# Picking the first pair's rows as rows: stationary slot matrix, one more turn, and row stores from other buffers

## The chip, the cores and the metric

The kernel runs on one core of one Trainium2 chip. The metric is device time in microseconds (us) of one execution; lower is better. Before the change it is 1299.22 us, the median of 3 runs (1299.15 to 1299.3).

The engines go by the profile's names. PE is TensorE (matmuls; its weight loads are listed as PEld), DVE is VectorE, ACT is ScalarE, POOL is GpSimd, SP is SyncE, which here only issues DMAs. ACTq and SPq are the instruction streams of ACT and SP as far as they issue DMAs. A matmul has a stationary operand, which is loaded into the array, and a moving one, which streams through it. PSUM is the memory that PE writes into.

## The reference, cut to what matters

One decoder layer over a sequence of 512 tokens of width 1024, in float32. Four token mixers run on one input projection, their outputs are gated, merged and put through an output projection, and the residual is added. Then comes a mixture of experts: 4 groups of 8 experts; each token goes to 2 experts of one group.

```
x = x + gate1 * (merged @ w_out)                 # end of the mixer half
h = rms_norm(x) * (1 + scale2) + shift2          # input of the experts
group  = argmax(h @ w_router_group)              # 1 of 4
e1, e2 = top 2 of the 8 experts of that group    # with softmax gates
y = sum over e1, e2 of  gate_e * w_down_e(silu(h @ w_gate_e) * (h @ w_up_e))
x = x + gate2 * y
```

Each of the 32 experts has 6 MB of float32 weights, 198 MB in all, and each is read once whatever the routing.

## The kernel before, in words

Tokens are four blocks of 128 (t = 0 to 3), and `xm` holds the residual, 128 tokens by 1024 columns a block. Two stages touch the change.

**The output projection and the router** (L1271 to L1309) go in two halves of two blocks each (half 0: t = 0, 1; half 1: t = 2, 3). A half makes four column blocks of 256 columns (n = 0 to 3). Each has 48 matmul records `mm` in split precision (high and low parts of weights and activations, `wh`, `wl`, made by ACT at L253 and DVE at L254), then DVE multiplies by the gate into one of two buffers `yo` (L1290), adds it to `xm` (L1291; in half 0 POOL does that), and ACT squares the sum for the norm (L1293, `yo` being its scratch output). `logits` (L1256) then turns the block with four transposes `z` (L1260), ACT copies them from PSUM to `xT` (L1263) and PE makes the router's logits `pl`. In half 1 the products of column blocks 2 and 3 use weights kept from half 0; those of 0 and 1 are converted again.

**`route(half)`** (L1141) starts when a half's logits are there. It first writes normalised rows of x to a scratch in DRAM, `xhd`, from which later pairs gather their tokens: ACT scales `xm` into a buffer (L1157) and issues the store (L1158). Block i = 0 goes through `xg[0]` in one 512 KB store; block i = 1 goes through `yo[0]` and `yo[1]` in two stores of 256 KB. Then DVE works out group, experts, ranks and gates in a long chain of small operations. In half 1, when all 512 tokens are known, it ends with the tables of the first expert pair: `tb` and `tg` are matmuls that turn tokens into slots, `toki` holds the token number of each slot, `gx` the gates. From the last logits of half 1 on PE's order is the written one, and in `route(1)` DVE's is too; elsewhere the scheduler sets both.

**`pick`** (L1111) makes the tokens of pair 0 by matmul, straight from `xm`, so that no store and no gather stand before it. The slot matrix `rp` has, for each slot (64 per expert, 128 per pair), the norm factor at its token. A matmul has 128 columns of `xm` as the stationary operand (every fourth of 512) and `rp` as the moving one; the result is already turned (features by slots) in PSUM, `pt0`. It is called for blocks 0 and 1 in `meanwhile()`, a generator that fills PE's waiting spots in `route(1)` together with dummy matmuls `scr`, and for blocks 2 and 3 at the end, between `tb` and `tg`.

**The experts.** 16 pairs of experts follow. `turn_in(p)` transposes the gathered rows `xg[p % 2]` (L1357) for every pair but the first, whose `pt0` is ready, and scales them into `xe` (L1364, L1366). `front(p)` multiplies with the first two weight matrices (`ph`), `Back` with the third (`py`). `fetch(p)` (L1133) is the indirect DMA on POOL that gathers the rows of pair p. The weights come on SP's queue in loads of 1 MB through a ring of 20 buffers; a load waits until PE is done with the tile that its buffer held. DMAs issued from SP and ACT share eight completion semaphores in turn, so that a load can also wait for the DMA that used its semaphore before, row stores included.

Of the kernel before, what the change touches and what calls it, by code (L numbers as in the profile page):

```python
# [9 lines left out]
F32 = mybir.dt.float32  # L10
# [5 lines left out]
AF = mybir.ActivationFunctionType  # L16
# [5 lines left out]
D = 1024  # L22
KD = D // 128
NT = S // 128
# [8 lines left out]
WARM = (1, 0, 0, 2)  # L33
# [4 lines left out]
def trunk(ctx, tc, x, c, ada_w, ada_b, norm1_g, norm2_g, w_in, hgrn_lb, hgrn_norm_g, conv_w, conv_b, conv_ln_g,  # L38
# [3 lines left out]
    V, A, P, T = nc.vector, nc.scalar, nc.gpsimd, nc.tensor  # L42
# [14 lines left out]
    def mm(o, l, r, start, stop):  # L57
        T.matmul(o, l, r, start=start, stop=stop, skip_group_check=True)  # L58
# [12 lines left out]
    def psm(nm="mm"):  # L71
        return ps_mm.tile([128, 512], F32, name=nm, tag="mm")

    def psz(nm="z2"):
        return ps_z.tile([128, 2, 512], F32, name=nm, tag="z2")
# [194 lines left out]
    a = A.activation(wh[:, 4:], raw[:, 4:], AF.Copy)  # L270
# [690 lines left out]
    xm = keep.tile([128, NT, D], F32, name="xm")  # L961
# [44 lines left out]
    nr = nrm.enter_context(tc.tile_pool(name="nr", bufs=1))  # L1006
    yo = [nr.tile([128, 2, 256], F32, name="yo", bufs=2) for _ in range(2)]
# [26 lines left out]
    xg = [kp.tile([128, D], F32, name="xg0")]  # L1034
# [54 lines left out]
    def stream():  # L1089
        for i in range(len(order)):  # L1090
            load_to(i + len(ring))
            yield loaded[i]
# [15 lines left out]
            V.tensor_tensor(oh, iob, bc(idx), op=OP.is_equal)  # L1108
        return mx, idx, oh

    def pick(ts, ds):  # L1111

        for d in ds:
            a, k = divmod(d, 4)
            for t in ts:
                mm(pt0[:, d], xm[:, t, a * 512 + k:(a + 1) * 512:4], rp[t // 2][:, t % 2], t == 0 and k == 0, t == NT - 1)

    def meanwhile():


        scr = psm("scr")
        for n, ds in zip(WARM, ((), range(4), range(4, 8), ())):
            for _ in range(n):
                mm(scr, ident, xm[:, 0, :512], True, True)
            pick((0, 1), ds)
            a = yield
            if a is not None:
                mm(scr[:a.shape[-1], :2], a, ident[:, :2], True, True)
        yield

    def fetch(p):

        P.indirect_dma_start(out=xg[p % 2], out_offset=None, in_=xhd[:, :],  # L1133
                             in_offset=bass.IndirectOffsetOnAxis(ap=toki[:, p:p + 1], axis=0),
                             bounds_check=S - 1, oob_is_err=False)
# [3 lines left out]
    oR, ev, gv, cr, rp, pt0 = [], [], [], [], [], None  # L1139

    def route(half, pl, between=None):  # L1141

        then = between or (lambda a: None)
        ts = slice(2 * half, 2 * half + 2)
# [6 lines left out]
            V.scalar_tensor_tensor(lg[:, i], pl[:, i * 36:(i + 1) * 36], r[:, i:i + 1], crow, op0=OP.mult, op1=OP.add)  # L1151
        for i in range(2):
            t = 2 * half + i
            for cs, xs in ((slice(0, D), xg[0]),) if not i else ((slice(0, 512), yo[0]), (slice(512, D), yo[1])):
                if i:
                    xs = xs.rearrange("p a b -> p (a b)")
                A.activation(xs, xm[:, t, cs], AF.Copy, scale=r[:, i:i + 1])  # L1157
                nc.scalar.dma_start(xhd[t * 128:(t + 1) * 128, cs], xs)  # L1158
        gm, gi, og = first_max(lg[:, :, :4], 4, "f0")
# [13 lines left out]
        v2, i2, _ = first_max(eg, 8, "f2", False)  # L1173
# [10 lines left out]
        for i in range(2):  # L1184
            t = 2 * half + i
# [17 lines left out]
        if half:  # L1203
            tb = psm("tb")
            by_slot(tb[:, :16], lambda h, k_, i, j: ev[h][:, k_, i, j::2])
            slots0(1)
            pick((2, 3), range(8))
            V.tensor_scalar(toki, tb[:, :16], 1024.0, None, op0=OP.add)
            V.tensor_scalar(tok, tb[:, :16], 1024.0, None, op0=OP.add)

# [35 lines left out]
    def by_slot(o, what, first=True):  # L1246

        n = 0
        for h in range(2):
            for k_ in range(2):  # L1250
                for i in range(2):
                    for j in range(2):
                        mm(o[64 * j:64 * j + 64], oR[h][:, k_, i], what(h, k_, i, j), first and n == 0, n == 7)
                    n += 1
# [18 lines left out]
    for half in range(2):  # L1273
        pl = ps_o.tile([128, 512], F32, name="pl", tag="o1")
        ts = slice(2 * half, 2 * half + 2)
        cbs = (0, 1, 2, 3) if half == 0 else (2, 3, 0, 1)
        for n, cb in enumerate(cbs):
            if half == 0 or cb < 2:
                wo[cb] = wblock(w_out, 0, KD, cb * 256, 256)
            w = wo[cb]  # L1280
            if half and n == 3:
                load_to(EWX)
            cs = slice(cb * 256, cb * 256 + 256)
            o = psm()
            for i in range(2):
                three(o[:, i * 256:(i + 1) * 256],
                      tuple((lambda k, a=a: a[:, k, i * 128:(i + 1) * 128]) for a in (mh[half], ml[half])),
                      tuple((lambda k, a=a: a[:, k, :]) for a in w), KD, first=i == 0)
            y = yo[n % 2]
            V.tensor_mul(y, o.rearrange("p (t c) -> p t c", t=2), g1b[:, None, cs].to_broadcast([128, 2, 256]))  # L1290
            (V if half else P).tensor_add(xm[:, ts, cs], xm[:, ts, cs], y)  # L1291
            for i in range(2):
                A.activation(y[:, i], xm[:, 2 * half + i, cs], AF.Square,  # L1293
                             accum_out=sq2[:, 2 * half + i, cb:cb + 1])
            if n:
                logits(half, pl, n - 1, cbs[n - 1])
        between = None
        if half:
            pt0 = psz("xT").rearrange("p a (b c) -> p (a b) c", c=128)
            pe_order.enter_context(tc.manual_schedule(engines={mybir.EngineType.PE}))  # L1300
            between = meanwhile()
        logits(half, pl, 3, cbs[3], between)
        if half:
            with tc.manual_schedule(engines={mybir.EngineType.DVE}):
                slots0(0)
                next(between)
                route(half, pl, between.send)
        else:
            route(half, pl)  # L1309
# [36 lines left out]
    xg.append(moe.tile([128, D], F32, name="xg1", bufs=1))  # L1346
    P.memset(xg[1], 0.0)
    fetch(1)
    fetch(2)
    ew = stream()  # L1350

    def turn_in(p):

        pt = psz("xT").rearrange("p a (b c) -> p (a b) c", c=128) if p else pt0
        for d in range(KD) if p else ():
            a, k = divmod(d, 4)
            T.transpose(pt[:, d], xg[p % 2][:, a * 512 + k:(a + 1) * 512:4], ident)  # L1357
        if 0 < p < 14:
            fetch(p + 2)
        yield  # L1360
        xe = moe.tile([128, KD, 128], F32, name="xe", bufs=1)
        for d in range(KD):
            if d % 2 and not p:
                V.tensor_scalar(xe[:, d], pt[:, d], a2s[:, d:d + 1], sh2s[:, d:d + 1], op0=OP.mult, op1=OP.add)  # L1364
            else:
                A.activation(xe[:, d], pt[:, d], AF.Identity, scale=a2s[:, d:d + 1], bias=sh2s[:, d:d + 1])  # L1366
        yield xe
# [149 lines left out]
    b, xe = None, list(turn_in(0))[1]  # L1517
    for p in range(16):
# [10 lines left out]
        late_, b = b, Back(p, g)  # L1529
# [6 lines left out]
        xe = next(nxt, None)  # L1536
# [33 lines left out]
```

## Time and profile before

| what | value |
|---|---|
| median of 3 runs | 1299.22 us (1299.15 to 1299.3) |
| profiled execution, its own time | 1303.05 us |
| its span on the core | 1301.3 us |
| mean granted PE clock | 0.987 |
| PE busy | 1235.8 us (95%) |
| DVE / ACT / POOL busy | 674.9 / 483.3 / 209.9 us |
| DMA traffic | 299.04 MB, 230 GB/s over the span |

The profile is that of one execution, 3.83 us longer than the median of the runs; 1.75 us of its time lie outside the span. Its times count from the start of the span. A row of the timeline has start, duration, engine, line and operation, output<-inputs, sizes and count, and in brackets how long the engine sat idle before it and what released it. A row of a view by windows has its stretch and length, the busy time of PE, PEld, DVE, ACT and POOL with their instruction counts, the granted PE clock (1.00 is full, 2.4 GHz; 0.50 is 1.2 GHz), the busy share of the DMA engines and GB/s. The chain of waits has start, duration and what the end was waiting for. A group of instructions has busy time, mean of one in ns, and idle time before it with its releaser.

### The profile page before, as it was taken

How to read it: one execution, taken by the hardware profiler on the slowest of the kernel's cores; microseconds unless marked ns; L12 is line 12 of the kernel's file. 1: busy time of each engine (PE TensorE's matmuls, PEld its weight loads, DVE VectorE, ACT ScalarE, POOL GpSimd, SP SyncE). 2: the span in 40 equal slices, each digit the busy share in tenths (PEclk: the TensorE clock that was granted, in tenths of full speed). 3: DMA queues.
4: the chain of work that ended last, by engine and by line, in shares of the span. 5: the costliest groups of instructions: out<-in, count | busy, mean ns of one | idle time of the engine just before them, and what ended most of it. 6: DMA issues, size and time to landing. Idle time of an engine off the chain costs nothing.

```text
span 1301.3 us, 17173 instructions
## 1 busy us (share of the span) xinstructions
PE 1235.8 (95%) x6856; PEld 867.8 (67%) x6856; DVE 674.9 (52%) x1053; ACT 483.3 (37%) x727; POOL 209.9 (16%) x170
## 2 busy tenths in 40 slices
PE   7999998999999999998999997989999999899997
PEld 5789897987779987787888897634334433333334
DVE  2724679998964564458865444325333423232224
ACT  3447565446554465453434442112111211111110
POOL 3225846201110111122211110000000000000000
PEclk9999998999999999999999998999999999999999
DMA  9432211131222322236875297699999999999995
GB/s 328 147 112 66 97 48 52 33 97 65 88 75 65 98 65 86 77 102 202 260 223 188 88 390 259 242 420 418 419 420 419 419 419 420 419 419 420 419 413 197
DMA packets 108624, 299.04 MB, mean 230 GB/s; under 512 B 9646, under 2 KB 65054, under 8 KB 84732
## 3 DMA queue, kind: packets, MB, share of 16 engines
q1 hardware_dynamic: 102312, 289.45, 58.6%
q10 hardware_dynamic: 3588, 4.36, 1.0%
q0 software_dynamic: 2640, 4.09, 0.9%
q8 instruction: 55, 0.90, 0.3%
q14 instruction: 29, 0.24, 0.1%
HBM read 297.56 MB, written 4.20 MB: 232 GB/s over the span
## 4 chain that ended last, share of the span: by engine, by line
PE 59%; DMA 26%; DVE 5%; ACT 4%; POOL 2%; issue 2%; ACTq 0%; SPq 0%; POOLq 0%; DVEq 0%
PE mm L58 39%; DMA ew<-in_expert_w_dram 24%; PE ph L58 6%; PE py L58 3%; PE z L58 2%; PE po L58 1%; PE xT L58 1%; PE sbe L58 1%; DVE wl L254 1%; DMA adaw<-in_ada_w_dram 1%; POOL sf L577 1%; DMA xhd<-yo 1%; ACT wh L253 1%; PE sbz L58 1%; POOL hgf L578 1%
## 5 line engine op out<-in xcount | busy, mean ns | idle before, releaser
L58 PE MATMUL ph<-ew,xe 128*64 128x512 f32 x1024 | 233.1, 594 | 18.7 <-DMA ew<-in_expert_w_dram 17.9
L58 PEld LDWEIGHTS ph<-ew,xe 128*64 128x64 f32 x1024 | 77.0, 137 | 171.5 <-issue 128.9
L58 PE MATMUL mm<-hh,wh 128*128 128x512 f32 x448 | 178.9, 399 | 0.0
L58 PE MATMUL mm<-hh,wl 128*128 128x512 f32 x448 | 174.9, 390 | 1.6 <-DVE wl L266 1.6
L254 DVE TENSOR_TENSOR wl<-raw,wh 128x2048 fp32r<-128x2048 f32 x55 | 131.8, 2396 | 83.7 <-ACT wh L253 83.7
L58 PE MATMUL mm<-hl,wh 128*128 128x512 f32 x448 | 174.8, 390 | 0.0
L1434 DVE TENSOR_TENSOR xm<-xm,po 128x512 f32<-128x512 f32 (+1 forms) x136 | 81.8, 648 | 170.0 <-PE po L58 169.8
L58 PE MATMUL mm<-wh,hh 128*128 128x256 f32 x448 | 131.4, 293 | 0.0
L253 ACT ACTIVATE wh<-raw 128x2048 fp32r<-128x2048 f32 x55 | 105.1, 1911 | 69.7 <-PE mm L58 69.5
L58 PE MATMUL mm<-wl,hh 128*128 128x256 f32 x448 | 128.4, 287 | 0.0
L58 PE MATMUL mm<-wh,hl 128*128 128x256 f32 x448 | 128.2, 286 | 0.0
L58 PE MATMUL py<-ew,gT 128*64 128x512 f32 (+1 forms) x544 | 113.9, 570 | 1.3 <-ACT gT L1401 1.3
L58 PEld LDWEIGHTS mm<-hh,wh 128*128 128x128 f32 x448 | 84.2, 188 | 23.3 <-issue 7.2
L58 PEld LDWEIGHTS mm<-hh,wl 128*128 128x128 f32 x448 | 84.1, 188 | 19.9 <-DVE wl L266 1.9
L58 PEld LDWEIGHTS mm<-hl,wh 128*128 128x128 f32 x448 | 84.2, 188 | 16.5 <-DVE hl L206 0.3
L58 PEld LDWEIGHTS mm<-wh,hh 128*128 128x128 f32 x448 | 87.5, 195 | 6.0 <-issue 5.8
L58 PEld LDWEIGHTS mm<-wl,hh 128*128 128x128 f32 x448 | 87.7, 196 | 0.2
L58 PEld LDWEIGHTS mm<-wh,hl 128*128 128x128 f32 x448 | 87.5, 195 | 0.0
L58 PEld LDWEIGHTS py<-ew,gT 128*64 128x64 f32 x544 | 37.5, 137 | 69.1 <-issue 64.8
L1380 ACT ACTIVATE g<-ph 128x512 f32<-128x512 f32 x16 | 9.6, 598 | 190.6 <-PE ph L58 190.6
L1133 POOL DMA_INDIRECT xg<-xhd,toki x15 | 15.1, 1004 | 396.5 <-PE xT L1357 341.9
L157 ACT ACTIVATE yh<-py 128x512 fp32r<-128x512 f32 (+1 forms) x34 | 19.4, 572 | 140.4 <-DVE py L1422 135.2
(441 smaller groups left out, 2075.2 us busy)
## 6 DMA issues: line engine op xcount, KB each, us to landing
ew<-in_expert_w_dram SPq DMA_DIRECT2D x186, 1024.0 KB, 19.9
raw<-in_w_in_dram SPq DMA_DIRECT2D x26, 1024.0 KB, 5.0
raw<-in_w_gate_dram SPq DMA_DIRECT2D x16, 1024.0 KB, 5.5
adaw<-in_ada_w_dram SPq DMA_DIRECT2D x64, 256.0 KB, 3.3
aw<-in_ada_w_dram SPq DMA_DIRECT2D x32, 256.0 KB, 5.4
raw<-in_w_branch_dram SPq DMA_DIRECT2D x8, 1024.0 KB, 5.6
raw<-in_w_out_dram SPq DMA_DIRECT2D x6, 1024.0 KB, 5.9
ew<-in_expert_w_dram SPq DMA_DIRECT2D x12, 512.0 KB, 12.2
```

The source lines that it names most:

```text
L58: T.matmul(o, l, r, start=start, stop=stop, skip_group_check=True)
L157: A.activation(h_ap, src, AF.Copy)
L253: a = A.activation(wh, raw, AF.Copy)
L254: v = V.tensor_sub(wl, raw, wh.bitcast(F32))
L577: P.tensor_add(vw(sf)[:, :, 0], vw(sf)[:, :, 0], tb(1))
L578: P.tensor_add(vw(f)[:, :, 1], vw(f)[:, :, 1], tb(0))
L1133: P.indirect_dma_start(out=xg[p % 2], out_offset=None, in_=xhd[:, :], in_offset=bass.IndirectOffsetOnAxis(ap=toki[:, p:p + 1], axis=0), bo ...
L1380: A.activation(g, ph[:, 0], AF.Sigmoid)
L1434: V.tensor_add(xm[:, t, cs], xm[:, t, cs], po)
```

## The change

Three things are edited.

1. `pick` has the slot matrix as the stationary operand and 512 whole columns of `xm` as the moving one: 2 matmuls for each block of tokens instead of 8. The result is rows (slots by features). ACT copies one half of them to `xg[0]` and DVE the other, and pair 0 then takes the same way through `turn_in` as the other pairs: eight transposes.
2. `fetch(2)`, which writes `xg[0]`, is issued behind the transposes of pair 0.
3. The row stores of half 0 both go through `xg[0]`, one after the other. Those of half 1 go through `yo[0]` and `yo[1]` for i = 0, and through two buffers `xT` for i = 1: four stores of 256 KB.

```diff
-    def pick(ts, ds):
-        for d in ds:
-            a, k = divmod(d, 4)
+    def pick(ts, cols=(0, 1)):
+        for c in cols:
             for t in ts:
-                mm(pt0[:, d], xm[:, t, a * 512 + k:(a + 1) * 512:4], rp[t // 2][:, t % 2], t == 0 and k == 0, t == NT - 1)
+                mm(pt0[:, c], rp[t // 2][:, t % 2], xm[:, t, c * 512:c * 512 + 512], t == 0, t == NT - 1)
...
-        for n, ds in zip(WARM, ((), range(4), range(4, 8), ())):
+        for n, cs in zip(WARM, ((), (0,), (1,), ())):
...
-            for cs, xs in ((slice(0, D), xg[0]),) if not i else ((slice(0, 512), yo[0]), (slice(512, D), yo[1])):
-                if i:
-                    xs = xs.rearrange("p a b -> p (a b)")
+            parts_ = (xg[0],)
+            if half:
+                parts_ = [nr.tile([128, 512], F32, name="xT", bufs=2) for _ in range(2)] if i else [a.rearrange("p a b -> p (a b)") for a in yo]
+            for n, xs in enumerate(parts_):
+                n_ = D // len(parts_)
+                cs = slice(n * n_, n * n_ + n_)
                 A.activation(xs, xm[:, t, cs], AF.Copy, scale=r[:, i:i + 1])
                 nc.scalar.dma_start(xhd[t * 128:(t + 1) * 128, cs], xs)
...
-            pick((2, 3), range(8))
+            pick((2, 3))
+            A.activation(xg[0][:, :512], pt0[:, 0], AF.Copy)
+            V.tensor_copy(xg[0][:, 512:], pt0[:, 1])
...
-            pt0 = psz("xT").rearrange("p a (b c) -> p (a b) c", c=128)
+            pt0 = psz("xe")
...
     fetch(1)
-    fetch(2)
...
-        pt = psz("xT").rearrange("p a (b c) -> p (a b) c", c=128) if p else pt0
-        for d in range(KD) if p else ():
+        pt = psz("xT").rearrange("p a (b c) -> p (a b) c", c=128)
+        for d in range(KD):
...
-        if 0 < p < 14:
+        if p < 14:
             fetch(p + 2)
```

How the orders move, at three places. On ACT, behind the first logits of half 0 and into half 1; `xg_5967` is `xg[0]`, `wh` the converted weights of half 1, `z_6459` the transposes of its first column block. Before:

```order
L1157 ACTIVATE xg_5967<-xm,rr 128x1024
L1157 ACTIVATE yo<-xm,rr 128x512
L1158 DMA xhd<-xg_5967 128x1024
L1158 DMA xhd<-yo 128x512
L1157 ACTIVATE yo<-xm,rr 128x512
L1163 ACTIVATE ge<-ge 128x8
L1214 ACTIVATE dv<-dv 128x2
L1158 DMA xhd<-yo 128x512
L253 ACTIVATE wh<-raw 128x2048
L1293 ACTIVATE yo,sq_5981<-xm 128x256 x2
L253 ACTIVATE wh<-raw 128x2048
L1263 ACTIVATE xT<-z_6459 128x512
```

After:

```order
L1159 ACTIVATE xg_5967<-xm,rr 128x1024
L1165 ACTIVATE ge<-ge 128x8
L1160 DMA xhd<-xg_5967 128x1024
L1218 ACTIVATE dv<-dv 128x2
L253 ACTIVATE wh<-raw 128x2048
L1159 ACTIVATE xg_5967<-xm,rr 128x1024
L1297 ACTIVATE yo,sq_5981<-xm 128x256
L1160 DMA xhd<-xg_5967 128x1024
L1297 ACTIVATE yo,sq_5981<-xm 128x256
L253 ACTIVATE wh<-raw 128x2048
L1297 ACTIVATE yo,sq_5981<-xm 128x256 x2
L1267 ACTIVATE xT<-z_6457 128x512
```

The second write of `xg[0]` stands behind the first weight conversion, and waits for the first store to have read `xg[0]`; `yo` is no longer a source of stores here. Behind that write stand the squares, the second conversion and the copy `xT` of the first column block.

On PE, from the last logits of half 1 on, where `pick` for blocks 0 and 1 stands; `f0o` and `f1o` are results of DVE that release `meanwhile()`. Before:

```order
L58 MATMUL pl<-wr,xT 128x36 x4
L58 MATMUL xT<-g1b,xm 128x128 x8
L58 MATMUL scr<-ident,f0o 4x2
L58 MATMUL xT<-g1b,xm 128x128 x8
L58 MATMUL scr<-ident,f1o 8x2
L58 MATMUL scr<-xm,ident 128x512 x2
```

After:

```order
L58 MATMUL pl<-wr,xT 128x36 x4
L58 MATMUL xe<-xm,g1b 128x512 x2
L58 MATMUL scr<-ident,f0o 4x2
L58 MATMUL xe<-xm,g1b 128x512 x2
L58 MATMUL scr<-ident,f1o 8x2
L58 MATMUL scr<-xm,ident 128x512 x2
```

Eight matmuls have become two at each place; a matmul in float32 leaves two records in the trace. Blocks 2 and 3 go from 16 to 4 in the same way, and eight transposes stand behind `tg`, ahead of the first `ph`.

On DVE, near the end of `route(1)`; `g1b` is where the slot matrix is made. Before:

```order
L1241 TENSOR_TENSOR g1b<-orr,c__6732 128x256 x2
L1243 TENSOR_TENSOR g1b<-g1b 128x256
L1208 TENSOR_SCALAR toki<-tb 128x16
L1209 TENSOR_SCALAR tok<-tb 128x16
L1211 TENSOR_REDUCE gs<-ge 128x2
```

After:

```order
L1245 TENSOR_TENSOR g1b<-orr,c__6722 128x256 x2
L1247 TENSOR_TENSOR g1b<-g1b 128x256
L1211 COPY xg_5967<-xe 128x512
L1212 TENSOR_SCALAR toki<-tb 128x16
L1213 TENSOR_SCALAR tok<-tb 128x16
L1215 TENSOR_REDUCE gs<-ge 128x2
```

The copy of the picked rows stands between the slot matrix and `toki`; behind `toki` come the gates and `gx`, which `tg` needs.

## Rows read from the trace of the kernel before

**Rows 1.** View by windows of two stretches: before the first pair, and the tail.

```profile
821.00:837.00 16.00, 13.49 (x107) 10.05 (x107) 6.84 (x28) 2.09 (x6) 3.13 (x3) 0.89 0.34 122
...
850.00:1240.00 390.00, 371.77 (x1699) 151.56 (x1701) 130.08 (x259) 70.82 (x165) 12.02 (x13) 1.00 1.01 419
```

**Rows 2.** The chain of waits: the first of its pieces in the tail.

```profile
953.98 20.51 DMA ew<-in_expert_w_dram
```

**Rows 3.** Timeline from the stores of half 0 into half 1.

```profile
775.79 0.36 ACTq L1158 DMA_DIRECT2D xhd<-xg  x1
...
784.21 11.82 SPq L1086 DMA_DIRECT2D ew<-in_expert_w_dram  x3
...
787.77 0.69 DVE L1290 TENSOR_TENSOR yo<-mm,g1b 128x512 f32<-128x512 f32 x1 [6.63 <-DMA xhd<-yo]
...
789.22 0.42 ACT L1293 ACTIVATE yo<-xm 128x256 f32<-128x256 f32 x1 [8.45 <-DVE xm L1291]
...
789.29 1.09 PE L1260 MATMUL z<-ident,xm 128*128 128x128 f32 x4 [4.61 <-issue]
...
790.03 1.89 ACT L253 ACTIVATE wh<-raw 128x2048 fp32r<-128x2048 f32 x1
...
799.99 0.60 PE L1260 MATMUL z<-ident,xm 128*128 128x128 f32 x4
```

**Rows 4.** View by windows: four stretches of different granted clocks.

```profile
593.54:600.00 6.46, 4.56 (x23) 3.83 (x23) 6.46 (x5) 3.11 (x4) 3.24 (x2) 1.00 0.32 104
...
788.60:795.20 6.60, 4.51 (x20) 4.24 (x21) 6.53 (x10) 4.10 (x10) 0.00 (x0) 0.50 0.41 138
...
795.20:808.00 12.80, 12.57 (x106) 12.15 (x105) 2.75 (x5) 1.64 (x6) 0.00 (x0) 1.00 0.57 196
...
826.00:829.50 3.50, 3.50 (x17) 3.50 (x16) 0.62 (x4) 0.00 (x0) 1.16 (x1) 0.51 0.27 80
```

**Rows 5.** Timeline from the last logits of half 1 to the second pair.

```profile
811.73 3.98 PE L58 MATMUL xT<-g1b,xm 128*128 128x128 f32 x16
...
819.82 1.98 PE L58 MATMUL scr<-xm,ident 128*128 128x512 f32 x4
...
821.64 0.18 PE L58 MATMUL pl<-ohb,trib 128*128 128x32 bf16 x1
...
824.25 0.17 DVE L1208 TENSOR_SCALAR toki<-tb 128x16 int32<-128x16 f32 x1
...
824.39 7.74 PE L58 MATMUL xT<-g1b,xm 128*128 128x128 f32 x32 [0.96 <-DVE g1b L1243]
...
826.17 0.49 DVE L1227 TENSOR_TENSOR gx<-oe,gh 128x128 f16<-128x128 f16 x2
...
832.05 0.68 PE L58 MATMUL tg<-gx,orr 128*64 128x16 f16 x32
...
833.33 1.08 PE L58 MATMUL ph<-ew,xe 128*64 128x512 f32 x4 [0.60 <-ACT xe L1366]
...
837.43 11.10 SPq L1086 DMA_DIRECT2D ew<-in_expert_w_dram  x8
...
847.64 1.23 PE L1357 MATMUL xT<-ident,xg 128*128 128x128 f32 x8
```

**Rows 6.** Groups of instructions by shape, 808 to 850.

```profile
L58 PE MATMUL xT<-g1b,xm 128*128 128x128 f32 x64 | 15.7, 410 | 1.0 <-DVE g1b L1243 1.0
...
L1263 ACT ACTIVATE xT<-z 128x512 f32<-128x512 f32 x2 | 1.2, 597 | 5.6 <-PE z L1260 5.6
...
L1157 ACT ACTIVATE xg<-xm,rr 128x1024 f32<-128x1024 f32 x1 | 1.1, 1150 | 0.8 <-DVE rr L148 0.8
```

**Rows 7.** DMA issues: size, median us from issue to landing.

```profile
ew<-in_expert_w_dram SPq DMA_DIRECT2D x186, 1024.0 KB, 19.9
...
xhd<-yo ACTq DMA_DIRECT2D x4, 256.0 KB, 11.1
...
xg<-xhd,toki POOLq DMA_INDIRECT x15, 9.1
```

More of the change, by code (lines that the diff above doesn't have):

```diff
@@ L1109, in first_max @@
         return mx, idx, oh
-    def pick(ts, ds):
-        for d in ds:
-            a, k = divmod(d, 4)
+    def pick(ts, cols=(0, 1)):
+        for c in cols:
             for t in ts:
-                mm(pt0[:, d], xm[:, t, a * 512 + k:(a + 1) * 512:4], rp[t // 2][:, t % 2], t == 0 and k == 0, t == NT - 1)
+                mm(pt0[:, c], rp[t // 2][:, t % 2], xm[:, t, c * 512:c * 512 + 512], t == 0, t == NT - 1)
     def meanwhile():
         scr = psm("scr")
-        for n, ds in zip(WARM, ((), range(4), range(4, 8), ())):
+        for n, cs in zip(WARM, ((), (0,), (1,), ())):
             for _ in range(n):
                 mm(scr, ident, xm[:, 0, :512], True, True)
-            pick((0, 1), ds)
+            pick((0, 1), cs)
             a = yield
```

## The prediction, made before the changed kernel ran

> **What bounds the kernel now.** I read the tail first, by windows: from 850 to 1240 the DMA engines are busy at 1.01 and move 419 GB/s [rows 1]. The chain of waits says the same: from 953.98 on it consists of weight loads of some 20 us, one behind the other [rows 2]. So the end is set by how early the weight stream can run freely. Before the tail stands a stretch in which it can't: between 821 and 837 the DMA share is 0.34 [rows 1], because the ring is full, and SP issues the next loads only at 837.43, when the first pair's `ph` has released the first tile [rows 5]. Bytes and rate behind that point don't change, so each us by which the first `ph` comes earlier should come off the end, and what has to be costed is the path up to the first `ph` at 833.33 [rows 5].
>
> Two stretches of that path meet the change. The first is half 1: DVE's multiply into `yo` waits 6.63 us for a row store out of `yo`, PE then stands idle for 4.61 us until the transposes at 789.29 [rows 3], and PE's clock is at 0.50, its level of 1.2 GHz, from 788.60 to 795.20 [rows 4]. The second is the route of half 1, from the first `pick` at 811.73 to 833.33, 21.60 us. `pick` itself is 64 records and 15.7 us busy there [rows 6].
>
> **Stores of half 0 (A).** They no longer read `yo`, so DVE's stall goes and PE does its transposes when it gets to them, at 784.7 (789.29 less 4.61), until 785.4. Late next is ACT: it writes `xg[0]` a second time, for which the first store must have landed. That store was issued at 775.79, and SP, which waited for it, went on at 784.21 [rows 3]: 8.4 us. In the new order only an operation of 0.2 us stands ahead of the issue, so I take 784.4. Behind the wait stand the copy (1.15 us [rows 6]), a pair of squares (0.81, from 789.22 to 790.03 [rows 3]), the conversion `wh` (1.89 [rows 3]), another pair of squares (0.81) and the copy `xT` (0.60 [rows 6]): 5.3, with hand-overs and the issue of the store 5.8. So `xT` is there at 790.2. PE has 24 products in the meantime; at full clock 106 records took 12.57 us [rows 4], 0.118 each, so it runs out at 785.4 + 2.8 = 788.2 and idles 2.0 us. Then come the 8 records of `pl` (1.0 with its hand-over, at the same rate) and 24 more products (2.8), and the next transposes start at 794.1 where they were at 799.99 [rows 3]: A = -5.9 us. An idle stretch of 1.90 us elsewhere left the clock at 1.00 [rows 4], so I charge none here. Bounds: without the wait -7.7 (PE would not idle); if the store lands as late as those from `yo`, 11.1 us [rows 7], PE idles as long as before and all but 2.6 of the gain may go at full clock, or all of it at half clock.
>
> **The picked rows (B).** Up to 821.64, where `pl<-ohb` starts, the 21.60 us hold two groups of `pick` of 16 records (3.98 us for the first), then dummies; then 2.75 until the second `pick` starts at 824.39; 7.66 until `tg` at 832.05; 1.28 until `ph` [rows 5]. In the new form a group of 16 records of 128 columns is one of 4 records of 512. The nearest row is the dummies: the same shape, 4 records from 819.82 to 821.64, 1.82 us [rows 5], against 3.98 less some overlap, 3.92. The two groups save 4.2, the second `pick` becomes 8 records, 3.64, and saves 4.0.
>
> The price stands at the end. When `pick` is done, ACT copies one half (0.60 for 128x512 out of PSUM [rows 6]), DVE the other, and waits for ACT's first (0.69, as the multiply at 787.77 [rows 3]). Behind DVE's copy in its written order wait `toki` and the gates, and behind those `tg`: from 824.25 to the end of `gx` at 826.66 it is 2.41 us [rows 5], which `pick` covered before. Then most of `tg` (0.5 of its 0.68), eight transposes (1.23 [rows 5]), the first `xe` with its hand-over (0.6, which is 1.28 less 0.68), and 0.2 for the hand-overs between: 6.2 in place of 1.28, or +4.9. B = -4.2 - 4.0 + 4.9 = -3.3 at full clock, 18.3 us for the route.
>
> PE idles some 3.9 us between `pick` and `tg` here, close to the 4.61 after which the clock was at half, so I expect half clock behind it. `tg` and transposes would cost about 1 more; `ph` runs at (847.64 - 833.33)/64 = 0.22 a record [rows 5] and at half clock at 0.45, and some 16 records lie before the first release, partly bound by `xe`: +1.2 is what I take. Sum +2.2, bounds 0 and +5.0 (the second `pick` at half clock too, since the clock was at 0.51 from 826.00 to 829.50 [rows 4], 1.9 more, and `ph` entirely bound). B = -1.1, bounds -3.3 and +1.7.
>
> *A page against this change.* A record of `pick` takes 0.23 us (7.66 for the 32 ahead of `tg`), one of the wide dummies 0.455: twice as long for four times the columns. The Trainium skill, "TensorE: Matmul & The Clock Gate", section "Back-to-back issue gap", has the gap between matmuls of a stream grow with their moving columns; these are 4096 in both forms (32 times 128, 8 times 512), so by that rule `pick` would save next to nothing. The rows differ from it, and I go by them.
>
> **At nothing.** `fetch(2)` moves behind pair 0's transposes, and `fetch(1)` stays behind it on POOL. `fetch(1)` is issued some 2 us behind the first `ph` at the latest, lands about 9.1 us later [rows 7], and is needed 14.3 us behind the first `ph`, where pair 1's transposes stand [rows 5]: cover 3 us or more, beyond which pair 1 would be delayed one for one. The four stores of half 1 are issued some 4 us into the route and land about 11.1 us later [rows 7], 15 us in; the first `xe` of ACT, which takes over the room of their buffers, comes 17.8 us in (18.3 less 0.5): cover 3 us, and behind that each us of the stores is one of the first `ph`. SP's loads wait for other semaphores than before; the DMA engines have 0.34 of 16 us of work ahead of the first release [rows 1], so some 10 us are free there to fill the ring in. Half 0's matmuls for the ranks come some products later, and nothing of half 1 waits for them.
>
> **Sum.** -5.9 - 1.1 = -7.0. The profiled execution took 1303.05, of which 1.75 lie outside its span, so it would be 1296.0; the median of the runs is 3.83 below the profiled one, which gives 1292.2.
>
> **Rivals.**
> - The clock stays up behind `pick`. For it: the copies and `tg` break the idle stretch into pieces. Against: 4.61 us of idle in half 1 did bring it down. Then -5.9 - 3.3 = -9.2: 1290.0.
> - The wait moves from DVE to ACT. The first store lands 11.1 us after its issue, at 787.1; `xT` is there at 792.9, PE idles 4.7 us as before, its clock falls, and `pl` and 24 products take 7.6 instead of 3.8: transposes at 800.5 or, at full clock, 796.7. For it: the other stores did take that long. Against: the very same store took 8.4. A about 0, with B -1.1: 1298.1, no change that can be told.
> - Slower, by the same place: the first store lands among the weight loads as they do, up to 19.9 us [rows 7]. Each us that it comes behind 787.1 delays half 1 by one. To be slower by over 2.6 us in all, A has to be +3.7, a landing at about 790.3, 14.5 us after the issue; halfway to 19.9, at 793.1, A is +6.5 and the time 1304.6. For it: the weight loads go through the same DMA engines at that time. Against: the same store took 8.4, those of `yo` 11.1.
> - `pick` gains nothing: wide records at the rate per column of the narrow ones. B = -3.3 + 8.2 + 2.2 = +7.1, with A +1.2: 1300.4, no change. Against it is the dummies' row, which has the same shape. By the rule of the Trainium skill above it would come out so.
>
> **How the numbers follow.** Forecast 0.66, clock up 0.14, ACT's wait 0.11, late store 0.05, no gain in `pick` 0.04. What a measurement of this kernel can tell from no change is about 0.2%, 2.6 us. The first two are faster: 0.80; the third and most of the last the same: 0.14; the late store and a little of the last slower: 0.06. The forecast's own range reaches from -7.7 - 3.3 (1288.2) to -5.9 + 1.7 (1295.0); to leave out no more than 2 in 10 I let it reach ACT's wait: 1288 to 1298.5.
>
> **What would show it.** Right: no wait of DVE for `xhd` in half 1, a wait of ACT for it of some 3 us instead, transposes of half 1's second column block 9.4 us behind those of the first (794.1 less 784.7), where it was 10.7; records of `pick` at 0.45; an idle PE of about 4 us ahead of `tg` and a granted clock of 0.50 behind it; SP's first load after the full ring at about 830 instead of 837.4, and a tail of the same length at 419 GB/s. The forecast would be wrong if the first load came 7 us earlier and the end did not (then the tail has another limit), or if PE in half 1 waited for `xT` longer than 4 us.

## The result and the profile after

The changed kernel takes 1294.32 us (median of 18 runs, 1290.15 to 1298.32) against 1299.92 us of the kernel before (18 runs, 1298.32 to 1307.24). The ratio is 0.9949, its 95% interval 0.9935 to 0.9962, so 4.9 to 8.4 us less. The forecast was 1292.2 in a range of 1288 to 1298.5.

The profiled executions differ by more, 1301.3 and 1290.0 us of span, and not all of that is the change's. The place at which the two programs part is half 0's route; its norm factor `rr` (L148) is made at 774.41 before and at 770.61 after, by the same instructions. So I count from `rr`. The kernel before, timeline:

```profile
774.41 0.16 DVE L148 TENSOR_TENSOR rr<-rs_y,rs_z 128x2 f32<-128x2 f32 x1
```

The kernel after, the same row, and behind it half 1:

```profile
770.61 0.16 DVE L148 TENSOR_TENSOR rr<-rs_y,rs_z 128x2 f32<-128x2 f32 x1
...
771.99 0.36 ACTq L1160 DMA_DIRECT2D xhd<-xg  x1
...
780.45 1.15 ACT L1159 ACTIVATE xg<-xm,rr 128x1024 f32<-128x1024 f32 x1 [3.59 <-DMA xhd<-xg]
...
785.05 0.58 ACT L1267 ACTIVATE xT<-z 128x512 f32<-128x512 f32 x1
...
785.68 1.08 PE L58 MATMUL pl<-wr,xT 128*128 128x36 f32 x8 [1.60 <-ACT xT L1267]
...
789.49 0.60 PE L1264 MATMUL z<-ident,xm 128*128 128x128 f32 x4
```

The first store is issued at 771.99 and ACT's second write of `xg[0]` gets its release 8.4 us later: the wait of 6.63 us on DVE [rows 3] has become one of 3.59 us on ACT, and what is left of PE's 4.61 us of idle time is 1.60. The transposes of half 1's second column block start 18.88 us behind `rr`; before it was 25.58 (799.99 [rows 3] less 774.41). That is A: -6.7 us.

The route of half 1 in the same trace:

```profile
801.24 1.96 PE L58 MATMUL xe<-xm,g1b 128*128 128x512 f32 x4
...
807.11 0.18 PE L58 MATMUL pl<-ohb,trib 128*128 128x32 bf16 x1
...
809.86 3.70 PE L58 MATMUL xe<-xm,g1b 128*128 128x512 f32 x8 [0.96 <-DVE g1b L1247]
...
813.59 0.60 ACT L1210 ACTIVATE xg<-xe 128x512 f32<-128x512 f32 x1 [8.49 <-PE xe L58]
...
814.22 0.69 DVE L1211 COPY xg<-xe 128x512 f32<-128x512 f32 x1 [4.42 <-ACT xg L1210]
...
816.76 0.49 DVE L1231 TENSOR_TENSOR gx<-oe,gh 128x128 f16<-128x128 f16 x2
...
817.09 0.55 PE L58 MATMUL tg<-gx,orr 128*64 128x16 f16 x24 [3.31 <-DVE gx L1231]
...
817.57 1.30 PE L1360 MATMUL xT<-ident,xg 128*128 128x128 f32 x8
...
819.47 2.75 PE L58 MATMUL ph<-ew,xe 128*64 128x512 f32 x6 [0.60 <-ACT xe L1369]
...
824.39 4.24 SPq L1086 DMA_DIRECT2D ew<-in_expert_w_dram  x4
```

Four wide records take 1.96 us, and the second `pick` takes 3.70 us where it took 7.74 [rows 5]. Behind it stand the two copies, one after the other, then DVE's chain up to `gx`, and PE idles for 3.31 us ahead of most of `tg`. From the first `pick` to the first `ph` it is 18.23 us instead of 21.60. Behind that the first release takes longer, 4.92 us instead of 4.10. By windows (second `pick`; from there to the first `ph`; from there to the first release; the tail):

```profile
809.86:813.56 3.70, 3.70 (x12) 1.51 (x14) 0.00 (x0) 0.00 (x0) 0.00 (x0) 1.00 1.02 340
...
813.56:819.47 5.91, 2.00 (x41) 1.66 (x41) 4.14 (x20) 1.26 (x3) 1.26 (x2) 0.93 0.29 114
...
819.47:824.39 4.92, 4.92 (x18) 1.60 (x20) 1.62 (x4) 2.66 (x4) 1.79 (x2) 0.74 0.42 108
...
850.00:1230.00 380.00, 361.99 (x1660) 148.25 (x1658) 128.59 (x257) 68.05 (x157) 11.91 (x12) 1.00 1.01 419
```

The granted clock is 1.00 for `pick` and 0.74 for the stretch to the release. So B is -3.37 + 0.82 = -2.55 us, and the first release comes 9.2 us earlier from `rr`: 53.78 instead of 63.02. The tail goes at 419 GB/s as before; from the first release to the last load's issue it is 438.02 us and was 437.82. After the last store of the output is issued the execution lasts 8.74 us in the one and 7.18 in the other; nothing of the change runs there, and this 1.6 us turns up and goes in the kernels below without regard to their edits. So the span counted from `rr` is 7.5 us shorter. The chain of waits ends in weight loads of some 20 us as it did [rows 2], the first of them at

```profile
1023.43 21.13 DMA ew<-in_expert_w_dram
```

where before it was at 953.98. Up to there it names PE, which has hardly a pause in this stretch, beside DMA engines at 1.01: rate and length of the tail are the same, but in its first part the chain does not tell which of the two sets the pace.

### The profile page after: what moved, and what is told of

It is laid out like the page before. It is cut to its first block, busy times and chain, and to the rows that moved or that the text cites. A ratio compares the mean times of both kernels' runs of the same rounds, so it can differ in the third digit from the quotient of the medians.

```text
span 1290.0 us, 17097 instructions
## 1 busy us (share of the span) xinstructions
PE 1224.9 (95%) x6816; PEld 851.8 (66%) x6816; DVE 674.9 (52%) x1054; ACT 484.2 (38%) x728; POOL 211.4 (16%) x170
## 5 line engine op out<-in xcount | busy, mean ns | idle before, releaser
L58 PE MATMUL ph<-ew,xe 128*64 128x512 f32 x1024 | 232.9, 597 | 18.3 <-DMA ew<-in_expert_w_dram 17.7
```

## The experiments

All times below are set against runs of the kernel before on the same chip. "From `rr`" is counted as above; each number is the difference of two starts in the timeline of that run's trace: the second column block's transposes, the first `pick`, the first `ph`, the first load that SP issues behind it.

The two kernels marked as one run (contiguous stationary, row columns 128) ran once each, and have no interval; the median of the kernel before on their chip was 1302.20 us.

| kernel | median us (runs) | ratio to before, 95% | 2nd block, from rr | pick to ph | ph to release | release, from rr |
|---|---|---|---|---|---|---|
| before | 1299.92 (18) | 1 | 25.58 | 21.60 | 4.10 | 63.02 |
| after | 1294.32 (18) | 0.9949, 0.9935 to 0.9962 | 18.88 | 18.23 | 4.92 | 53.78 |
| stores only | 1294.30 (9) | 0.9949, 0.9928 to 0.9971 | 18.96 | 21.59 | 4.10 | 56.40 |
| pick only | 1299.91 (12) | 0.9992, 0.9974 to 1.0009 | 25.46 | 18.17 | 5.07 | 60.44 |
| gates first | 1287.20 (6) | 0.9891, 0.9866 to 0.9916 | 20.18 | 15.08 | 3.68 | 50.68 |
| gates first, again | 1291.14 (6) | 0.9920, 0.9904 to 0.9936 | 20.31 | 16.77 | 3.68 | 52.70 |
| warm gap | 1290.78 (6) | 0.9914, 0.9889 to 0.9939 | 18.68 | 18.16 | 3.68 | 52.27 |
| own buffer | 1296.04 (12) | 0.9955, 0.9935 to 0.9975 | 22.41 | 18.17 | 5.14 | 57.47 |
| gates first, own buffer | 1292.58 (8) | 0.9933, 0.9911 to 0.9955 | 19.38 | 16.78 | 3.68 | 51.58 |
| xT store first | 1291.58 (6) | 0.9924, 0.9899 to 0.9950 | 18.05 | 20.04 | 4.69 | 54.53 |
| gates first, xT first | 1288.93 (6) | 0.9901, 0.9875 to 0.9927 | 18.07 | 16.72 | 3.68 | 50.26 |
| idle spots filled | 1286.25 (6) | 0.9891, 0.9872 to 0.9909 | 18.02 | 15.08 | 3.68 | 48.51 |
| contiguous stationary | 1294.89 (one run) | - | 25.77 | 14.21 | 3.68 | 55.41 |
| row columns 128 | 1297.77 (one run) | - | 20.18 | 20.28 | 4.54 | 56.75 |

**Stores only and pick only.** The first is the kernel before with the new stores, the second the changed kernel with the old ones.

> The kernel before with the new row stores alone (pick, its place and the first pair as before). My theory: the two parts add up. The stores carry -6.7 us of the path to the first ph, as the changed kernel's trace has it from the norm factors of half 0 (rr, L148) to the transposes of half 1's second column block: 25.6 us before, 18.9 after. So here about 18.9 us there, the route of half 1 unchanged at 21.6 us, the first release of the ring 6 to 7 us earlier from rr, and a time of about 1293.2 (ratio 0.995). Rival: the gain came from the way the two parts fall together, or the ring swallows a gain in half 1; then within 2 us of before, 1298 to 1300.

> The changed kernel with the row stores of before. My theory: half 1 has its stall on yo again (25.6 us from rr to the second column block's transposes), the route of half 1 takes 18.2 us instead of 21.6, the first ph's stretch to the first release 4.9 instead of 4.1; net -2.5 us: about 1297.4 (ratio 0.998). Rival (a matmul costs by its columns alone, 4096 in both forms): the route takes 25 us or more and the kernel is slower than before, 1303.

```diff
 # stores only: before, with
-            for cs, xs in ((slice(0, D), xg[0]),) if not i else ((slice(0, 512), yo[0]), (slice(512, D), yo[1])):
-                if i:
-                    xs = xs.rearrange("p a b -> p (a b)")
+            parts_ = (xg[0],)
+            if half:
+                parts_ = [nr.tile([128, 512], F32, name="xT", bufs=2) for _ in range(2)] if i else [a.rearrange("p a b -> p (a b)") for a in yo]
+            for n, xs in enumerate(parts_):
+                n_ = D // len(parts_)
+                cs = slice(n * n_, n * n_ + n_)
 # pick only: after, with these lines exchanged the other way round
```

In the traces the two add up: the first release comes 6.62 us earlier with the stores alone and 2.58 with `pick` alone, 9.20 together, and 9.23 in the changed kernel. With `pick` alone the stall on `yo` is back as it was:

```profile
783.09 0.69 DVE L1291 TENSOR_TENSOR yo<-mm,g1b 128x512 f32<-128x512 f32 x1 [6.64 <-DMA xhd<-yo]
...
784.61 1.09 PE L1261 MATMUL z<-ident,xm 128*128 128x128 f32 x4 [4.61 <-issue]
```

So in the path up to the first release neither part swallows the other. The second run's rival is out too, that the picked rows save nothing because the columns are as many: the route would have been 25 us and took 18.2. The times say less. That of `pick` alone can't be told from before (-3.4 to +1.2 us), and the stores alone have the same ratio, 0.9949, as the whole change: that the edit of `pick` makes the kernel faster is shown in the path of one trace each, not in the medians.

**What made the old records slow.** Two runs change `pick` itself. In the first the features come out in another order, so it computes something else than the reference.

> The kernel before with pick's stationary operand as 128 neighbouring columns of xm instead of every fourth of 512 (the features then come out in another order, so what is computed is not the reference's). It tells apart what made a record of pick take 0.233 us. If the stride of 16 bytes in the weight load is the cause: 0.11 to 0.15 us, as the contiguous pl and the transposes, pick's last 32 records 3.6 to 5 us and the kernel 8 us faster. If it is the number of weight loads, or the 128 moving columns in two passes: 0.23 us still.

> The changed kernel with pick's moving operand cut to 128 columns of xm a matmul (32 matmuls with the slot matrix stationary, as many columns in all as before and after, same result). If a matmul costs by its moving columns: 0.114 us a record, the last 32 records 3.7 us as the 8 wide ones. If each matmul has a floor of its own or waits for its weight load: 0.19 to 0.23 us a record, 6 to 7.4 us, and the kernel 5 us or more slower than the changed one.

```diff
 # contiguous stationary: before, with
-                mm(pt0[:, d], xm[:, t, a * 512 + k:(a + 1) * 512:4], rp[t // 2][:, t % 2], t == 0 and k == 0, t == NT - 1)
+                mm(pt0[:, d], xm[:, t, d * 128:d * 128 + 128], rp[t // 2][:, t % 2], t == 0 and k == 0, t == NT - 1)
 # row columns 128: after, with
-                mm(pt0[:, c], rp[t // 2][:, t % 2], xm[:, t, c * 512:c * 512 + 512], t == 0, t == NT - 1)
+                for q in range(0, 512, 128):
+                    mm(pt0[:, c, q:q + 128], rp[t // 2][:, t % 2], xm[:, t, c * 512 + q:c * 512 + q + 128], t == 0 and not q, t == NT - 1)
```

The weight loads of the kernel before, as a group by shape:

```profile
L58 PEld LDWEIGHTS xT<-g1b,xm 128*128 128x128 f32 x64 | 15.2, 328 | 1.1 <-DVE g1b L1243 1.1
```

Matmuls and weight loads of the contiguous one:

```profile
L58 PE MATMUL xT<-g1b,xm 128*128 128x128 f32 x64 | 7.9, 279 | 1.0 <-DVE g1b L1243 1.0
...
L58 PEld LDWEIGHTS xT<-g1b,xm 128*128 128x128 f32 x64 | 7.4, 192 | 1.1 <-DVE g1b L1243 1.1
```

The same 64 records are 7.9 us busy instead of 15.7 [rows 6], the mean weight load is 192 ns where the strided one was 328, and 16 of them take 2.03 us. Records of 128 columns with the slot matrix stationary take the same, 2.03 us for 16 at full clock; 4 wide ones take 1.96:

```profile
807.26 2.03 PE L58 MATMUL xe<-xm,g1b 128*128 128x128 f32 x16
```

So at full clock the cost does go by the columns, and the new form gains since its stationary operand lies contiguous, not since it is wide. The prediction's number for the wide records was right, its picture of why wasn't. (The last 32 records of 128 columns took 5.28 us, at a granted clock of 0.71.)

The contiguous one also shows a shorter way. It keeps the result turned, so it has neither copies nor transposes, and `tg` still finds its gates done: 14.21 us from the first `pick` to the first `ph`, where the changed form needs 18.2, and a first release 7.60 us ahead of the kernel before, where `pick` alone gave 2.58. There ACT's first `xe` waits for a row store out of `yo`, and PE for `xe` 1.01 us where it was 0.60:

```profile
824.88 0.46 ACT L1366 ACTIVATE xe<-xT,mod 128x128 f32<-128x128 f32 x1 [4.46 <-DMA xhd<-yo]
```

Whether the order of features that the rest of the kernel needs can be had with it was not tried.

**The wait for the gates, and the clock behind it.**

> The changed kernel with the two copies of the picked rows written behind the gates (behind gx, ahead of tg), so that DVE works out toki, gates and gx while PE still picks. My theory: behind pick stand only the two copies (1.3 us), the transposes (1.3) and the first xe with its hand-over (0.6): pick's end to first ph 3.3 instead of 5.9, route 15.6 us instead of 18.2; PE's idle stretch shrinks from 3.3 to about 1.4 us, the clock stays up and ph's first stretch is 4.1 again. In all some 3.4 us less than the changed kernel: 1291. Rival: the gates are hidden anyway, or the copies wait for something else (the landing of stores): same as the changed kernel, 1294.

> The changed kernel with four dummy matmuls of 512 columns (8 records, 3.6 us) between pick of blocks 2 and 3 and tg, where PE idles 3.3 us. My theory: the 0.8 us by which ph's stretch to the first release is longer than before (4.9 against 4.1) is PE's low clock behind that idle stretch; with the dummies the granted clock stays at 1.00, the stretch is 4.1, tg comes 0.3 us late: net -0.5 us, 1293.8, not to be told in time but in the trace. Rival: the 0.8 us is not the clock's (xe is late, DVE and ACT alternate); then 4.9 stays and the time is 0.3 us longer.

```diff
 # gates first: after, with the copies moved from behind pick((2, 3)) to ahead of tg
-            A.activation(xg[0][:, :512], pt0[:, 0], AF.Copy)
-            V.tensor_copy(xg[0][:, 512:], pt0[:, 1])
...
+            A.activation(xg[0][:, :512], pt0[:, 0], AF.Copy)
+            V.tensor_copy(xg[0][:, 512:], pt0[:, 1])
 # warm gap: after, with
             pick((2, 3))
+            for _ in range(4):
+                mm(psw, ident, xm[:, 0, :512], True, True)
```

With the gates first, DVE has `gx` done while PE still picks, and `tg` follows `pick` at once:

```profile
811.86 3.70 PE L58 MATMUL xe<-xm,g1b 128*128 128x512 f32 x8 [0.96 <-DVE g1b L1247]
...
813.65 0.48 DVE L1229 TENSOR_TENSOR gx<-oe,gh 128x128 f16<-128x128 f16 x2
...
815.49 0.68 PE L58 MATMUL tg<-gx,orr 128*64 128x16 f16 x32
...
815.60 0.60 ACT L1232 ACTIVATE xg<-xe 128x512 f32<-128x512 f32 x1 [3.25 <-PE xe L58]
...
816.23 0.69 DVE L1233 COPY xg<-xe 128x512 f32<-128x512 f32 x1 [2.09 <-ACT xg L1232]
...
818.32 6.23 PE L58 MATMUL ph<-ew,xe 128*64 128x512 f32 x28 [0.60 <-ACT xe L1369]
```

Route 15.08 us instead of 18.23, and 3.68 us to the release at a clock of 1.00. The dummies of the warm gap give the same 3.68 without touching the rest. So PE's low clock behind the idle 3.3 us cost 1.24 us (4.92 less 3.68). The rival, that `xe` is late there, is out. The other traces agree: in all five in which PE idles 3.31 us ahead of `tg` (after, `pick` only, own buffer, xT store first, row columns 128) the clock is at 0.71 to 0.81 up to the release, which takes 4.54 to 5.14 us; in the seven others with a changed `pick` or a changed order it is at 1.00 and takes 3.68. The kernel before needed 4.10 at full clock, and there `xe` is late: DVE has `pT` ahead of its first `xe`, and PE waits for it.

```profile
832.95 1.21 DVE L1394 TENSOR_SCALAR pT<-io,tok 128x512 fp32r<-128x512 f16 x1
...
834.16 0.40 DVE L1364 TENSOR_SCALAR xe<-xT,mod 128x128 f32<-128x128 f32 x1
...
834.61 13.10 PE L58 MATMUL ph<-ew,xe 128*64 128x512 f32 x60 [0.20 <-DVE xe L1364]
```

In the changed kernel `pT` runs at 817.96, beside the transposes, so 0.42 us of the 1.24 were won back there. In time the warm gap came out better than its trace explains: 1.5 us less to the release than the changed kernel, 3.5 in the medians, which come from different sets of runs.

But in half 1 the gates-first kernel lost 1.3 us to the changed one, with the same instructions in the same order. Its clock in the 8 us behind `pl`, and the changed kernel's:

```profile
786.15:794.15 8.00, 8.00 (x54) 7.82 (x55) 2.72 (x4) 1.50 (x5) 0.00 (x0) 0.79 0.84 305
```

```profile
785.68:793.68 8.00, 8.00 (x67) 7.82 (x68) 2.72 (x4) 1.51 (x5) 0.00 (x0) 1.00 0.96 363
```

PE had idled 1.38 us ahead of that in the one, 1.60 in the other. The same spot in the other traces with that wait: 1.69 and 1.40 us of idle, clock 1.00 (stores only, warm gap); 1.63 us and 0.79 (gates first again), 1.34 us and 0.79 (row columns 128).

**Taking that idle stretch away.**

> The changed kernel with the second block's row store of half 0 through the two xT buffers (two stores of 256 KB), so that ACT does not write xg[0] a second time and does not wait there for the first store. My theory: in the changed kernel that wait (3.6 us of ACT) leaves PE idle for 1.6 us in half 1. Here ACT waits only before xT of half 1's first column block, for a store issued some 2.4 us behind rr; landing 8.4 to 11.1 us later it lets pl start 0.9 to 1.6 us earlier: transposes of the second column block 17.3 to 18.0 us behind rr instead of 18.9, the time 1 to 1.6 us less than the changed kernel. Rival: the wait was hidden and PE is bound by wh and wl: 18.9 as before and no change in time.

> The copies behind the gates (as in the run with the gates first) and the second row store through the xT buffers. In the run with the gates first alone PE's idle stretch in half 1 was as long as in the changed kernel, but its clock fell behind it and half 1 lost 1.3 us. My theory: without that idle stretch half 1 takes 17.3 to 18.0 us from rr, its clock stays at 1.00, and the first release comes 2.2 to 2.9 us earlier than with the gates first alone, at 47.8 to 48.5 us behind rr: time 1285. Rival: the low clock in half 1 has nothing to do with that stretch and stays; then 1287.

> As the run with the second row store of half 0 in the xT buffers, but with these two stores issued ahead of that out of xg[0], some 1.3 us behind rr instead of 2.0 and 4.1. There the first of them landed 11.2 us behind its issue, PE idled 1.5 us for it, and the clock fell in one profile and not in the other. My theory: a store that is issued first lands about 8.4 us later, as the first one did in every trace so far; then xT is free at 9.7 us behind rr, ahead of the transposes at 10.1, PE does not idle in half 1, its clock stays at 1.00, and the second column block's transposes come 17.2 us behind rr. The time is 1.5 us less than the changed kernel, and its runs lie closer together. Rival: the time to landing belongs to stores in 2 KB pieces, 11.2 us whatever their place; then xT waits until 12.5 us behind rr, PE idles about 1.1 us, transposes at 18.3 us or, if the clock falls, 19 to 22.

> The gates ahead of the copies and the xT stores ahead of the other: the two improvements together. By my theory the first release comes 47.7 us behind rr (17.2 to the second column block, 11.7 to pick, 15.1 to the first ph, 3.7 to the release), 6.1 us ahead of the changed kernel in its profile: time 1286 to 1288. Rival (late landing, clock lottery in half 1): 48.8 to 52 us, no better than with the gates first alone.

```diff
 # own buffer: after, with
-            if half:
+            if half or i:
...
 # xT store first: that, and
-        for i in range(2):
+        for i in ((0, 1) if half else (1, 0)):
```

My theory of the first two fell. The wait only moved, from `xg[0]` to `xT`:

```profile
785.26 0.60 ACT L1267 ACTIVATE xT<-z 128x512 f32<-128x512 f32 x1 [1.06 <-DMA xhd<-xT]
...
785.91 1.59 PE L58 MATMUL pl<-wr,xT 128*128 128x36 f32 x8 [1.47 <-ACT xT L1267]
```

The store of 256 KB landed 11.2 us behind its issue at 773.95, PE idled 1.47 us, and its clock was at 0.57 over the next 8 us; with the gates first it was 1.56 us and 1.00. Hence 22.41 and 19.38 us to the second block: no gain, where I had expected 17.3 to 18.0. With the `xT` stores first PE idles 0.17 us there, and in both traces (and that of the filled one) the clock stays at 1.00:

```profile
785.14 1.08 PE L58 MATMUL pl<-wr,xT 128*128 128x36 f32 x8 [0.17 <-ACT xT L1267]
```

The second block comes at 18.05, not 17.2. `xT` is now behind the second `wh`, as ACT goes straight from the one into the other, and PE also waits 0.33 us for DVE's `wl` at 783.53. So this run doesn't tell when the store landed, only that it was before 784.5, at most 11.1 us behind its issue. Then the gain was lost again further on. The second `pick` took 5.3 us in both, as in the kernel with gates first and own buffer (5.4). The 5 us ahead of it and `pick` itself, with the gates first and the `xT` stores first:

```profile
808.35:813.35 5.00, 3.30 (x32) 1.59 (x31) 3.76 (x18) 0.21 (x1) 0.00 (x0) 0.99 0.99 371
...
813.35:818.68 5.33, 5.33 (x12) 2.14 (x14) 1.80 (x13) 0.20 (x1) 0.00 (x0) 0.69 0.92 325
```

The times of the two kernels that were to take 1285 and 1286 to 1288 us came out at 1292.58 and 1288.93. The `xT` stores first alone have a ratio of 0.9924 to the changed kernel's 0.9949, with intervals that overlap.

**Filling the idle spots ahead of the second pick.**

> The gates ahead of the copies, the xT stores first, and dummy matmuls in two places where PE waits ahead of the second pick (256 columns behind the matmuls for the ranks, 512 behind tb). In four traces, that of the two improvements together among them, the second pick took 5.3 us instead of 3.7 at a granted clock of 0.68 to 0.71, behind 5 us in which PE was busy 3.3; in the others it took 3.7 behind the same stretch. My theory: those idle spots are what lets the clock fall, and the wide records of the new pick pay for it, as the strided ones did not. With the spots filled the second pick takes 3.7 us again, 0.1 to 0.3 us later, and the first release comes 48.6 to 48.9 us behind rr instead of 50.3: time 1285 to 1287. Rival: the clock falls for another reason (what PE did earlier); then 5.3 and 50.4 as before, 1288 to 1289.

> The kernel with the gates first once more, beside the one above on the same chip, to see whether the rest of the additions is worth anything. My theory: 1287 as before, 1 us more than the filled one, which the intervals will hardly part; in the profile 50 to 52 us to the first release, with a low clock either in half 1 or at the second pick in about half of the executions. Rival: the additions cost what they give; then the same time or less than the filled one.

```diff
 # idle spots filled: gates first, xT store first, and
+        if half:
+            psw = psm("scr")
+            mm(psw[:, :256], ident, xm[:, 0, :256], True, True)
...
+            mm(psw, ident, xm[:, 0, :512], True, True)
             slots0(1)
             pick((2, 3))
```

The stretch ahead of the second `pick`, and `pick`:

```profile
806.36:811.36 5.00, 4.78 (x37) 2.12 (x36) 3.77 (x18) 0.21 (x1) 0.00 (x0) 1.00 0.97 354
...
811.36:815.06 3.70, 3.70 (x13) 1.51 (x14) 1.79 (x13) 0.20 (x1) 0.00 (x0) 1.00 1.02 328
```

PE is busy 4.78 of 5 us instead of 3.30, the second `pick` starts no later (8.62 us behind the first in all these kernels) and takes 3.70, and the first release comes at 48.51. The gates-first kernel beside it had its clock low in both places (0.79 in half 1, 0.68 in the second `pick`, 5.40 us) and needed 52.70. On that chip the medians are 1286.25 and 1291.14 (the gates-first kernel had 0.9891 in its first run, 0.9920 here). The filled kernel beats the kernel before by 1.1%, 0.9 to 1.3, where the changed one had 0.4 to 0.7, and it has the lowest median of those tried; but the gates-first kernel had the same ratio in its first run, so in time the two are not parted. Nor is it shown that the fillings kept the clock up: this is one trace, and of the ten with the new `pick` and unfilled spots five had 3.70 us there as well. Why one execution loses its clock in such a spot and another doesn't is not settled here.

## Why the prediction came out as it did

- **The limit.** Right: what came off the first release came off the issue of the last load, one for one. From the one to the other it is 437.7 to 438.5 us in all fourteen traces, whether the release came 2.6 or 14.5 us earlier. Behind the last load the end varies by some 1.6 us.
- **A, forecast -5.9, found -6.7.** The mechanism held: wait gone from DVE, ACT next. The landing of 8.4 us came as read off SP's wait. ACT's work from the landing to `pl` took 5.3 us, not 5.8; I had counted the store's issue and hand-overs as serial. No charge for the clock was right for that profile, but not as a rule: after 1.34 to 1.69 us of idle it fell in four of eight traces. Two of A's bounds do not follow from its own terms: without the wait the transposes come at 792.0 (785.4 and 2.8, 1.0 and 2.8), which is -8.0 and not -7.7, and with a landing after 11.1 us at full clock at 796.7, which leaves 3.3 of the gain and not 2.6.
- **B, forecast -1.1, found -2.55.** The route was 18.23 against 18.3 worked out, term by term: second `pick` 3.70 (3.64), copies 0.60 and 0.69, `toki` to the end of `gx` 2.42 (814.83 to 817.25; 2.41). The term that was mis-sized is the clock's: 2.2 forecast, 0.82 found against before. Eight of `tg`'s matmuls ran right behind `pick`, PE idled 3.31 us behind them and not 3.9, and the clock was low for only part of the way of `ph` to the release: 1.24 us, of which `pT`, now out of the way of `xe`, gave back 0.42. The bound that I named, the second `pick` at half clock, 1.9 us more, came true in five other traces with the new `pick`: 1.6 to 1.7.
- **The rivals.** ACT's wait took DVE's place, but the store landed 2.7 us ahead of what that rival needed; the late store didn't come, the first-issued store landed in 8.2 to 8.5 us in the traces that show it. `pick` did gain. That gain rested on the right number and the wrong reason, above. The Trainium skill's "Back-to-back issue gap" (page "TensorE: Matmul & The Clock Gate") has an isolated gap that goes by the columns, 134 cycles for 128 and 518 for 512. With that the contiguous records here agree, 2.03 us for 16 times 128 columns and 1.96 for 4 times 512, and the strided ones don't. The prediction took this for the rule of a stream; for a stream the section has about 81 and 131 ns, by which wide records save, and which the contiguous records don't bear out.
- **The edits at nothing.** The gathers, the half 1 stores and SP's lanes cost nothing that the tail shows; SP had the ring's last load issued at 810.19, 14 us ahead of the first release.
- **The time.** The sum was -7.0 us. In the profile the path gave 9.2 up to the release and 7.5 up to the end of the span, in the medians it was 5.6. That the median lies within 2.2 us of the forecast is partly luck: both terms came out larger than forecast in the profile, and the median shows no more than the stores alone. What each kernel takes up to `rr`, where nothing was changed, runs from 769.7 to 775.3 us in fourteen traces, so a few us of any one profile are not the edit's.

## What to carry to other kernels

Count a transfer's wait to its new owner: a buffer that is taken off one engine's hands puts the wait on the next, and only the trace says whether that one has slack. When an operation moves off PE's path, look at what it covered: here `pick` had hidden 2.4 us of gates, and putting the copies behind the gates instead of ahead took 3.15 us off the route in its first trace, about as much as the whole edit of `pick` (3.37). Before a new form is built around an operation that is slow, find out what makes it slow: here the stride of the old one's stationary operand. And in a stage that hangs on PE's clock, don't judge an edit by a single profile: the same `pick` took 3.70 us in some and 5.40 in others.

## What the runs showed of the hardware

- A weight load with a stride of 16 bytes took 328 ns against 192 for contiguous columns, and its matmul record 0.24 us against 0.12 (32 records ahead of `tg`: 7.74 and 3.84 us). The strided `pick` took 7.73 us at a granted clock of 0.78 (stores only) and at full clock 3.98 for half as many records, so it was no slower at the lower clock; the wide one took 3.70 at 1.00 and 5.40 at 0.68.
- Behind idle stretches of PE of 1.3 to 1.7 us in the same place the clock stayed at 1.00 in four traces and was low in four, which cost 1.4 to 3.1 us (from `pl` to the second block's transposes, against traces at full clock). Behind 3.31 us ahead of `tg` it was low in five of five.
- Of half 0's row stores the one of 512 KB that was issued first landed 8.2 to 8.5 us behind its issue. Those of 256 and 512 KB that were issued 0.6 to 3.1 us behind the first landed after 10.1 to 11.3 us; one of 512 KB issued 9.7 us behind it (gates first, again) after 7.5 us.
